# Skewness of 1024 rows: the last block's cubes written over their squares in PSUM, and the closing arithmetic moved from VectorE to ScalarE

## The chip, the cores and the metric

One NeuronCore of a Trainium2 chip. The metric is the device time of one execution in microseconds (us). A profiled execution gives a span, which is some 1.8 us shorter than the time, and a trace. Short names: PE is TensorE, DVE is VectorE, ACT is ScalarE, POOL is GpSimd. SBUF and PSUM are the core's two on-chip memories. A semaphore is a counter on which an instruction waits until another is done; a self-wait is such a wait of an engine for its own earlier instruction. An instruction that also gives a sum (accum_out) has a second record behind it in the trace, its accumulator read; the sum is ready when that ends. A pointer operand is a number per row, read from a 128x1 tile.

Ratios below are the mean time of one kernel's fast runs over the mean time of the kernel before in the same rounds on the same chip, with a 95% interval. They are not quite the ratio of the medians that stand beside them.

## The reference

```python
x = randn(1024, 8192)            # float32
mean = x.mean(-1, keepdims=True)
std  = x.std(-1, keepdims=True)
z = (x - mean) / (std + 1e-8)
out = (z ** 3).mean(-1)          # 1024 numbers
```

With the raw moments m1, m2, m3 (means of x, x^2, x^3) this is (m3 - 3 m1 m2 + 2 m1^3) / var^1.5, with var = m2 - m1^2. The kernel reads the 33.55 MB of x once.

## The kernel before

The rows lie in eight blocks of 128 partitions. Each block comes in several column units, each unit in one or more slices. For every slice ACT squares x and accumulates the sum of squares, and DVE multiplies the square by x and accumulates the sum of cubes. PE transposes x and adds it up, for the mean. From the last unit of block 6 on, the squares lie in PSUM in two buffers in turn (psq). The cube itself is wanted by nobody, only its sum, so it is written to a scratch tile called cube; in earlier blocks it goes over its square (sq).

```python
cube = small("cube", PS_MAX)                # one tile in SBUF
...
act(out=sq, in_=xt[:, s:e], func=AF.Square, scale=s_scale,
    accum_out=s2u[:, j : j + 1])
nc.vector.scalar_tensor_tensor(
    out=cube[:, 0 : e - s] if (b, k) >= PSUM_FROM else sq,
    in0=sq, scalar=1.0, in1=xt[:, s:e],
    op0=ALU.mult, op1=ALU.mult, accum_out=s3u[:, j : j + 1])
...
# the end, for block 7; p1 = m1 in PSUM
g.tensor_tensor(out=m2, in0=m2p, in1=s2u[:, j - 1 : j], op=ALU.add)
act(out=m1sq, in_=p1, func=AF.Square)
g.tensor_tensor(out=var, in0=m2, in1=m1sq, op=ALU.subtract)
g.tensor_tensor(out=rr, in0=var, in1=expo[:, 0:1], op=ALU.pow)
act(out=nm1, in_=p1, func=AF.Copy, scale=-3.0)
act(out=v3, in_=m1sq, func=AF.Identity, scale=1.0 / 3.0, bias=var)
nc.vector.tensor_reduce(out=num, in_=s3u[...block 7...], axis=X_AXIS, op=ALU.add)
nc.vector.scalar_tensor_tensor(out=num, in0=v3, scalar=nm1, in1=num,
                               op0=ALU.mult, op1=ALU.add)
nc.vector.tensor_tensor(out=skew[:, L:NB], in0=num, in1=rr, op=ALU.mult)
nc.sync.dma_start(out=ov, in_=skew)
```

The names in the trace drop digits: v3 is v_l, m2 is m_l, nm1 is nm_l, n3 is n_l there, num is num_l, and so on.

Of the kernel before, what the change touches and what calls it, by code (L numbers as in the profile page):

```python
# [9 lines left out]
AF = mybir.ActivationFunctionType  # L10
ALU = mybir.AluOpType
X_AXIS = mybir.AxisListType.X
# [12 lines left out]
PSUM_FROM = (6, 5)  # L25
SUB_MAX = 2304
PS_MAX, PS_BUFS = 1536, 2
# [12 lines left out]
def _plan(b, k):  # L40
    return _slices(UNITS[b][k], PS_MAX if (b, k) >= PSUM_FROM else SUB_MAX)


@with_exitstack
def kernel(
    ctx: ExitStack,
    tc: tile.TileContext,
    x: bass.AP,
    out: bass.AP,
):  # L50
    nc = tc.nc
    eng = mybir.EngineType
    ctx.enter_context(tc.manual_schedule(
        engines={eng.PE, eng.Activation, eng.DVE, eng.Pool, eng.SP}))
    P = nc.NUM_PARTITIONS
    R, C = x.shape
    NB = R // P
    L = NB - 1
    F = EARLY
    inv_n = 1.0 / float(C)  # L60
    s_scale = float(C) ** -0.5
    third = (1.0 / 3.0) ** 0.5
    assert len(UNITS) == NB and all(sum(u) == C for u in UNITS) and F == L


    xv = x.rearrange("(p b) c -> b p c", b=NB)
    ov = out.rearrange("(p b) -> p b", b=NB)


    n_sl = [sum(len(_plan(b, k)) for k in range(len(u))) for b, u in enumerate(UNITS)]  # L70
    K = max(n_sl)

    xpool = ctx.enter_context(tc.tile_pool(name="xp", bufs=X_BUFS))
    sqpool = ctx.enter_context(tc.tile_pool(name="sqp", bufs=SQ_BUFS))
    onep = ctx.enter_context(tc.tile_pool(name="onep", bufs=1))
    psq = ctx.enter_context(tc.tile_pool(name="psq", bufs=PS_BUFS, space=bass.MemoryType.PSUM))
    psum1 = ctx.enter_context(tc.tile_pool(name="ps1", bufs=1, space=bass.MemoryType.PSUM))

    def small(name, n):
        return onep.tile([P, n], FP, tag=name, name=name)  # L80

    onesn = small("onesn", 1)
    nc.vector.memset(onesn, inv_n)  # L83
    tiny = small("tiny", 1)
    nc.scalar.activation(out=tiny, in_=onesn, func=AF.Square)  # L85
    ident = small("ident", P)
    make_identity(nc, ident)
    s2u = small("s2u", NB * K)
    s3u = small("s3u", NB * K)
    nc.vector.memset(s2u, 0.0)  # L90
    nc.vector.memset(s3u, 0.0)
    cube = small("cube", PS_MAX)
    junk = small("junk", K)
    expo = small("expo", F)
    nc.gpsimd.memset(expo, -1.5)
    skew = small("skew", NB)
    m1a = small("m1a", F)
    tsb = small("tsb", P)

    tp = psum1.tile([P, P], FP, tag="tp", name="tp")  # L100
    s1ps = psum1.tile([P, NB], FP, tag="s1ps", name="s1ps")
    act, g = nc.scalar.activation, nc.gpsimd

    def close_first_blocks():

        m2, m3 = small("m2a", F), small("m3a", F)
        for dst, src in ((m2, s2u), (m3, s3u)):
            nc.vector.tensor_reduce(  # L108
                out=dst, in_=src[:, 0 : F * K].rearrange("p (b c) -> p b c", c=K),
                axis=X_AXIS, op=ALU.add,  # L110
            )
        m1sq, m1sq3, nm1 = small("m1sqa", F), small("m1sq3a", F), small("nm1a", F)
        act(out=m1sq, in_=m1a, func=AF.Square)
        act(out=m1sq3, in_=m1a, func=AF.Square, scale=third)
        act(out=nm1, in_=m1a, func=AF.Copy, scale=-3.0)
        var, rr = small("vara", F), small("rra", F)
        g.tensor_tensor(out=var, in0=m2, in1=m1sq, op=ALU.subtract)  # L117
        g.tensor_tensor(out=m1sq3, in0=m1sq3, in1=var, op=ALU.add)
        g.tensor_tensor(out=m1sq3, in0=m1sq3, in1=nm1, op=ALU.mult)
        g.tensor_tensor(out=m3, in0=m3, in1=m1sq3, op=ALU.add)  # L120
        g.tensor_tensor(out=rr, in0=var, in1=expo, op=ALU.pow)  # L121
        g.tensor_tensor(out=skew[:, 0:F], in0=m3, in1=rr, op=ALU.mult)

    for b, widths in enumerate(UNITS):
        c0 = 0
        j = b * K
        for k, w in enumerate(widths):
            last_unit = b == L and k == len(widths) - 1
            xt = xpool.tile([P, w], FP, tag="x", name=f"x_{b}_{k}")
            nc.sync.dma_start(out=xt, in_=xv[b, :, c0 : c0 + w])  # L130
            c0 += w
            n = w // P
            for c in range(n):
                nc.tensor.matmul(  # L134
                    out=tp, lhsT=xt[:, c * P : (c + 1) * P], rhs=ident,
                    start=(k == 0 and c == 0), stop=(c0 == C and c == n - 1),
                    is_transpose=True,
                )
            if last_unit:
                nc.scalar.copy(out=tsb, in_=tp)  # L140
            for s, e in _plan(b, k):
                if (b, k) >= PSUM_FROM:
                    sq = psq.tile([P, PS_MAX], FP, tag="psq", name=f"psq_{b}_{k}_{s}")[:, 0 : e - s]
                else:
                    sq = sqpool.tile([P, e - s], FP, tag="sq", name=f"sq_{b}_{k}_{s}")
                act(  # L146
                    out=sq, in_=xt[:, s:e], func=AF.Square, scale=s_scale,
                    accum_out=s2u[:, j : j + 1],
                )
                nc.vector.scalar_tensor_tensor(  # L150
                    out=cube[:, 0 : e - s] if (b, k) >= PSUM_FROM else sq,
                    in0=sq, scalar=1.0, in1=xt[:, s:e],
                    op0=ALU.mult, op1=ALU.mult, accum_out=s3u[:, j : j + 1],
                )
                j += 1
            if (b, k) == EARLY_AT:
                nc.scalar.copy(out=m1a, in_=s1ps[:, 0:F])
                close_first_blocks()
            if b == L and k == len(widths) - 2:
                m2p = small("m2p", 1)  # L160
                act(out=junk[:, 0 : n_sl[L] - 1], in_=s2u[:, L * K : j], func=AF.Copy,
                    accum_out=m2p)
        if b < L:
            nc.scalar.copy(out=tsb, in_=tp)  # L164
        nc.tensor.matmul(out=s1ps[:, b : b + 1], lhsT=tsb, rhs=onesn, start=True, stop=True)  # L165


    p1 = s1ps[:, L : L + 1]
    m1sq, nm1, v3, m2, var, rr, num = (
        small(f"{t}_l", 1) for t in ("m1sq", "nm1", "v3", "m2", "var", "rr", "num")  # L170
    )
    g.tensor_tensor(out=m2, in0=m2p, in1=s2u[:, j - 1 : j], op=ALU.add)
    act(out=m1sq, in_=p1, func=AF.Square)
    g.tensor_tensor(out=var, in0=m2, in1=m1sq, op=ALU.subtract)  # L174
    g.tensor_tensor(out=rr, in0=var, in1=expo[:, 0:1], op=ALU.pow)  # L175
    act(out=nm1, in_=p1, func=AF.Copy, scale=-3.0)
    act(out=v3, in_=m1sq, func=AF.Identity, scale=1.0 / 3.0, bias=var)  # L177
    nc.vector.tensor_reduce(out=num, in_=s3u[:, L * K : L * K + n_sl[L]], axis=X_AXIS, op=ALU.add)  # L178
    nc.vector.scalar_tensor_tensor(  # L179
        out=num, in0=v3, scalar=nm1, in1=num, op0=ALU.mult, op1=ALU.add  # L180
    )
    nc.vector.tensor_tensor(out=skew[:, L:NB], in0=num, in1=rr, op=ALU.mult)  # L182
    nc.sync.dma_start(out=ov, in_=skew)


# [28 lines left out]
```

## Time and profile before

| | before |
|---|---|
| time, median of 3 | 92.33 us (92.21 to 92.37) |
| span of the profiled run | 90.6 us |
| x has landed by | about 83.4 us |
| last cube's sum ready | 87.51 us |
| last DVE step ends | 88.30 us |

The prediction shows the lines. ACT waits for x for the last time at 78.76 us, PE at 83.41. From the fourth cube of block 7 (82.04 us) to the end DVE works without waiting for data, so that stretch is what a change of the tail can shorten.

### The profile page before, as it was taken

The page shows a single profiled execution, that of the slowest core. Times are in us where ns is not written, and L with a number is a line of the kernel's source. Part 1 is how long each engine was busy: PE and PEld are TensorE (multiplying, and loading weights), DVE is VectorE, ACT ScalarE, POOL GpSimd, SP SyncE. Part 2 cuts the span into 40 slices and gives each one's busy share as a digit, 9 for nine tenths or more (in the row PEclk, how much of TensorE's full clock was granted, in tenths as well). Part 3 has the DMA queues.
Part 4 walks back from the last instruction along what each step waited for, and adds up shares of the span by engine and source line. Part 5 has one row for each costly group of instructions (what it writes and reads, how often), then busy time and mean ns, then how long its engine had stood idle before and what let it go on. Part 6 is the DMA issues. An engine that isn't in the chain of part 4 may idle for free. (4 is left out here: it accounts for less than half of the span.)

```text
span 90.6 us, 1442 instructions
## 1 busy us (share of the span) xinstructions
PE 66.5 (73%) x528; PEld 60.2 (66%) x528; DVE 74.1 (82%) x92; ACT 69.1 (76%) x103; POOL 4.2 (5%) x16
## 2 busy tenths in 40 slices
PE   0003999988986959897589778989898798897700
PEld 0003999887975949686569667978687586776600
DVE  0000498969999799999988999999999989989980
ACT  6003969497885979897589889989888798898910
POOL 3000000000000000000000000000000000006440
PEclk9999999999999999999999999999999999999996
DMA  3999999999999999999999999999999999992000
GB/s 101 347 412 427 441 427 420 434 449 430 397 407 442 419 432 426 420 428 418 422 421 433 411 426 411 409 410 420 411 416 420 409 411 421 412 397 115 0 0 2
DMA packets 4614, 33.64 MB, mean 371 GB/s; under 512 B 640, under 2 KB 640, under 8 KB 3072
## 3 DMA queue, kind: packets, MB, share of 16 engines
q1 hardware_dynamic: 4608, 33.56, 89.4%
q8 instruction: 4, 0.07, 0.3%
q14 instruction: 2, 0.02, 0.0%
HBM read 33.55 MB, written 0.00 MB: 370 GB/s over the span
## 5 line engine op out<-in xcount | busy, mean ns | idle before, releaser
L134 PE MATMUL tp<-ident,x 128*128 128x128 f32 x512 | 64.0, 282 | 16.0 <-DMA x<-in_x_dram 15.8
L150 DVE SCALAR_TENSOR_TENSOR sq<-sq,x 128x2048 f32<-128x2048 f32 (+9 forms) x34 | 62.0, 1872 | 12.4 <-ACT sq L146 12.3
L134 PEld LDWEIGHTS tp<-ident,x 128*128 128x128 f32 x512 | 58.3, 146 | 20.3 <-DMA x<-in_x_dram 11.9
L146 ACT ACTIVATE sq<-x 128x2048 f32<-128x2048 f32 (+9 forms) x34 | 53.5, 1575 | 14.4 <-DMA x<-in_x_dram 12.6
L150 DVE SCALAR_TENSOR_TENSOR cube<-psq,x 128x1280 f32<-128x1280 f32 (+3 forms) x8 | 11.1, 1390 | 0.7 <-ACT psq L146 0.2
L146 ACT ACTIVATE psq<-x 128x1280 f32<-128x1280 f32 (+3 forms) x8 | 9.3, 1161 | 0.9 <-DVE cube L150 0.5
L146 ACT ACTIVATION_READ_ACCUMULATOR sq<-x 128x1 f32 x34 | 6.3, 186 | 0.0
L165 PEld LDWEIGHTS s1ps<-onesn,tsb 128*128 128x128 f32 x16 | 2.4, 188 | 5.2 <-ACT tsb L164 4.7
L165 PE MATMUL s1ps<-onesn,tsb 128*128 128x1 f32 x16 | 3.1, 260 | 3.4 <-ACT tsb L164 3.0
L117 POOL TENSOR_TENSOR vara<-m2a,m1sqa 128x7 f32<-128x7 f32 x1 | 0.2, 206 | 80.8 <-DVE m3a L108 80.8
L150 DVE DVE_READ_ACCUMULATOR sq<-sq,x 128x1 f32 x34 | 2.8, 82 | 0.0
L164 ACT COPY tsb<-tp 128x128 f32<-128x128 f32 x7 | 1.7, 250 | 1.3 <-PE tp L134 1.2
L85 ACT ACT_TABLE_LOAD x1 | 1.3, 1283 | 0.7 <-PEq L198 0.7
L121 POOL TENSOR_TENSOR rra<-vara,expo 128x7 f32<-128x7 f32 x1 | 1.5, 1507 | 0.0
L146 ACT ACTIVATION_READ_ACCUMULATOR psq<-x 128x1 f32 x8 | 1.5, 188 | 0.0
L83 DVE MEMSET onesn<- 128x1 f32 x1 | 0.1, 59 | 0.8 <-PEq L198 0.8
L150 DVE DVE_READ_ACCUMULATOR cube<-psq,x 128x1 f32 x8 | 0.7, 84 | 0.0
L177 ACT ACTIVATE v_l<-m1sq_l,var_l 128x1 f32<-128x1 f32 x1 | 0.3, 294 | 0.4 <-POOL var_l L174 0.4
L175 POOL TENSOR_TENSOR rr_l<-var_l,expo 128x1 f32<-128x1 f32 x1 | 0.6, 563 | 0.1
L179 DVE SCALAR_TENSOR_TENSOR num_l<-v_l,nm_l,num_l 128x1 f32<-128x1 f32 x1 | 0.2, 220 | 0.1
masks.py:199 POOL TENSOR_SCALAR_AFFINE_SELECT ident<-ident 128x128 f32<-128x128 f32 x1 | 0.3, 294 | 0.1
L140 ACT COPY tsb<-tp 128x128 f32<-128x128 f32 x1 | 0.3, 266 | 0.0
(27 smaller groups left out, 4.5 us busy)
## 6 DMA issues: line engine op xcount, KB each, us to landing
x<-in_x_dram SPq DMA_DIRECT2D x4, 2048.0 KB, 14.1
x<-in_x_dram SPq DMA_DIRECT2D x4, 1472.0 KB, 27.2
x<-in_x_dram SPq DMA_DIRECT2D x5, 640.0 KB, 9.3
x<-in_x_dram SPq DMA_DIRECT2D x4, 704.0 KB, 10.1
x<-in_x_dram SPq DMA_DIRECT2D x2, 960.0 KB, 19.8
x<-in_x_dram SPq DMA_DIRECT2D x2, 896.0 KB, 22.6
x<-in_x_dram SPq DMA_DIRECT2D x1, 1728.0 KB, 25.4
x<-in_x_dram SPq DMA_DIRECT2D x2, 768.0 KB, 15.2
```

Of the source, the lines that this page charges most:

```text
L85: nc.scalar.activation(out=tiny, in_=onesn, func=AF.Square)
L117: g.tensor_tensor(out=var, in0=m2, in1=m1sq, op=ALU.subtract)
L121: g.tensor_tensor(out=rr, in0=var, in1=expo, op=ALU.pow)
L134: nc.tensor.matmul(out=tp, lhsT=xt[:, c * P : (c + 1) * P], rhs=ident, start=(k == 0 and c == 0), stop=(c0 == C and c == n - 1), is_transp ...
L140: nc.scalar.copy(out=tsb, in_=tp)
L146: act(out=sq, in_=xt[:, s:e], func=AF.Square, scale=s_scale, accum_out=s2u[:, j : j + 1],)
L150: nc.vector.scalar_tensor_tensor(out=cube[:, 0 : e - s] if (b, k) >= PSUM_FROM else sq, in0=sq, scalar=1.0, in1=xt[:, s:e], op0=ALU.mult, ...
L164: nc.scalar.copy(out=tsb, in_=tp)
L165: nc.tensor.matmul(out=s1ps[:, b : b + 1], lhsT=tsb, rhs=onesn, start=True, stop=True)
L175: g.tensor_tensor(out=rr, in0=var, in1=expo[:, 0:1], op=ALU.pow)
L177: act(out=v3, in_=m1sq, func=AF.Identity, scale=1.0 / 3.0, bias=var)
L179: nc.vector.scalar_tensor_tensor(out=num, in0=v3, scalar=nm1, in1=num, op0=ALU.mult, op1=ALU.add)
```

## The change

It means to shorten the tail at both ends. Cubes of block 7 (and the last of block 6) go over their squares, so the scratch tile and the waits of DVE for itself disappear. And DVE keeps one step behind the last cube instead of three: ACT adds up the earlier cube sums (n3) and forms num = -3 m1 v3 + n3, and DVE finishes with (last sum + num) * rr. To make room on ACT the partial sum of squares moves one unit earlier, at the price of one more addition on POOL.

```diff
-    cube = small("cube", PS_MAX)
...
-                    out=cube[:, 0 : e - s] if (b, k) >= PSUM_FROM else sq,
+                    out=sq,
...
-            if b == L and k == len(widths) - 2:
+            if b == L and k == len(widths) - 3:
                 m2p = small("m2p", 1)
-                act(out=junk[:, 0 : n_sl[L] - 1], in_=s2u[:, L * K : j], func=AF.Copy,
+                act(out=junk[:, 0 : n_sl[L] - 2], in_=s2u[:, L * K : j], func=AF.Copy,
                     accum_out=m2p)
...
+    g.tensor_tensor(out=m2p, in0=m2p, in1=s2u[:, j - 2 : j - 1], op=ALU.add)
     g.tensor_tensor(out=m2, in0=m2p, in1=s2u[:, j - 1 : j], op=ALU.add)
...
-    nc.vector.tensor_reduce(out=num, in_=s3u[:, L * K : L * K + n_sl[L]], axis=X_AXIS, op=ALU.add)
-    nc.vector.scalar_tensor_tensor(
-        out=num, in0=v3, scalar=nm1, in1=num, op0=ALU.mult, op1=ALU.add
+    n3 = small("n3_l", 1)
+    act(out=junk[:, 0 : n_sl[L] - 1], in_=s3u[:, L * K : j - 1], func=AF.Copy, accum_out=n3)
+    act(out=num, in_=v3, func=AF.Identity, scale=nm1, bias=n3)
+    nc.vector.tensor_scalar(
+        out=skew[:, L:NB], in0=s3u[:, j - 1 : j], scalar1=num, scalar2=rr,
+        op0=ALU.add, op1=ALU.mult,
     )
-    nc.vector.tensor_tensor(out=skew[:, L:NB], in0=num, in1=rr, op=ALU.mult)
```

## The prediction

> **What bounds the kernel now.** I read the page first, for where the engines stand.
>
> ```profile
> span 90.6 us, 1442 instructions
> PE 66.5 (73%) x528; PEld 60.2 (66%) x528; DVE 74.1 (82%) x92; ACT 69.1 (76%) x103; POOL 4.2 (5%) x16
> DMA  3999999999999999999999999999999999992000
> GB/s 101 347 412 427 441 427 420 434 449 430 397 407 442 419 432 426 420 428 418 422 421 433 411 426 411 409 410 420 411 416 420 409 411 421 412 397 115 0 0 2
> ```
>
> The DMA row is the one to see: 35 slices of 2.27 us full, at about 420 GB/s, and then nothing. No engine reaches that. So until about 83.5 us the arrival of x sets the pace, and work saved on DVE before then is lost in a wait for data. What a tail change can move is the stretch after the last landing, roughly 83.4 to 90.6 us. Second, the timeline of that stretch (columns: start, duration, engine, line, operation, tiles, then idle before it and who ended it).
>
> ```profile
> 82.04 1.48 DVE L150 SCALAR_TENSOR_TENSOR cube<-psq,x 128x1280 f32<-128x1280 f32 x1
> 83.62 1.49 DVE L150 SCALAR_TENSOR_TENSOR cube<-psq,x 128x1280 f32<-128x1280 f32 x1
> 84.74 0.19 ACT L146 ACTIVATION_READ_ACCUMULATOR psq<-x 128x1 f32 x1
> 85.19 0.27 ACT L140 COPY tsb<-tp 128x128 f32<-128x128 f32 x1
> 85.21 1.49 DVE L150 SCALAR_TENSOR_TENSOR cube<-psq,x 128x1280 f32<-128x1280 f32 x1
> 85.36 0.61 ACT L146 ACTIVATE psq<-x 128x512 f32<-128x512 f32 x1
> 85.89 0.19 ACT L146 ACTIVATION_READ_ACCUMULATOR psq<-x 128x1 f32 x1
> 86.65 0.29 ACT L177 ACTIVATE v_l<-m1sq_l,var_l 128x1 f32<-128x1 f32 x1 [0.45 <-POOL var_l L174]
> 86.70 0.56 POOL L175 TENSOR_TENSOR rr_l<-var_l,expo 128x1 f32<-128x1 f32 x1
> 86.80 0.69 DVE L150 SCALAR_TENSOR_TENSOR cube<-psq,x 128x512 f32<-128x512 f32 x1
> 87.42 0.08 DVE L150 DVE_READ_ACCUMULATOR cube<-psq,x 128x1 f32 x1
> 87.54 0.16 DVE L178 TENSOR_REDUCE num_l<-s3u 128x1 f32<-128x7 f32 x1
> 87.82 0.22 DVE L179 SCALAR_TENSOR_TENSOR num_l<-v_l,nm_l,num_l 128x1 f32<-128x1 f32 x1
> 88.14 0.16 DVE L182 TENSOR_TENSOR skew<-num_l,rr_l 128x1 f32<-128x1 f32 x1
> 88.33 0.35 SPq L183 DMA_DIRECT2D out_dram<-skew  x1
> ```
>
> DVE sets the end. The last four cubes start at 82.04, 83.62, 85.21 and 86.80, with no stall but a small gap before each. Then three tiny steps run from 87.54 to 88.30, the output is issued at 88.33, and 2.3 us later the span ends. The square of the last unit is there at 86.08 (85.89 + 0.19), 0.72 us before its cube begins, so ACT has slack. The chain of waits agrees: nothing but DVE.
>
> To price the gap I looked at cubes of the same width in an earlier block, where the cube already overwrites its square.
>
> ```profile
> 54.02 1.48 DVE L150 SCALAR_TENSOR_TENSOR sq<-sq,x 128x1280 f32<-128x1280 f32 x1
> 55.43 1.48 DVE L150 SCALAR_TENSOR_TENSOR sq<-sq,x 128x1280 f32<-128x1280 f32 x1
> 56.85 0.08 DVE L150 DVE_READ_ACCUMULATOR sq<-sq,x 128x1 f32 x1
> ```
>
> Start to start is 1.41 us there, against 1.58 to 1.59 in block 7, though the instruction lasts the same 1.48 to 1.49. The instruction streams say why. All cubes of block 7 write one tile, cube, so each carries a wait on DVE's own semaphore for the one before it. Cubes that write sq carry none, and begin under the end of their predecessor. So the self-wait costs 1.59 - 1.41 = 0.18 us.
>
> **What the Trainium skill says.** "VectorE: DVE Perf Modes", section "The DRAIN you can't avoid", reports that eight copies take the same 13.88 us with a semaphore after each as with one after the last. By that the self-wait would be free. This trace differs (1.59 against 1.41 us), and I follow the trace. "Perfetto Trace Analysis", section "Optimizing Scalar/DVE Operations", gives a DVE access overhead of about 60 ns on SBUF and 125 ns on PSUM. For a PSUM read the trace hardly shows it (1489 ns mean from psq, 1484 ns from sq, both 1280 wide); no cube writes PSUM yet, so up to 65 ns more each is an open estimate. "PSUM — Partial Sum Buffer", section "PSUM bank collisions raise a hardware error", forbids two engines in one bank at a time. A psq buffer is 1536 x 4 bytes, three of that page's 2 KiB banks, so ACT's buffer and DVE's share none; on one engine reading and writing the same bank the section is silent, and so is this trace. "ScalarE: Activation LUTs", section "What ACT_TABLE_LOAD costs", adds about 93 ns for each per-partition scale or bias operand, and lets neighbours overlap by about 93 ns. The trace: v3 with one such operand took 294 ns, its neighbours without one 163 and 173; and the three small squares and copies from 80.31 on start 0.12, 0.10 and 0.09 us apart at 190 to 208 ns each. It agrees within some 30 ns.
>
> **The change, part by part.**
>
> Part one, cubes over squares. Seven self-waits vanish, those of block 7 (0.18 x 7 = 1.26 us of DVE time at most). I walk it. The first cube of block 7 can begin at 75.49 + 1.41 = 76.90 instead of 77.08. The second is held by its square, ready at 78.40, so 78.42 instead of 78.53. The third waits for its square, which waited for the DMA (78.76 to 80.24), so 80.26 as before: what was gained is lost here. The two reductions of the closing of blocks 0 to 6 follow at 81.81 and 81.93, without waits, and the fourth cube stays at 82.04. From here DVE is behind its squares. Fifth: 82.04 + 1.41 = 83.45 (before 83.62). Sixth: 83.45 + 1.41 = 84.86, but its square ends its accumulator read at 84.93, so 84.95 (before 85.21). Seventh: 84.95 + 1.41 = 86.36 (before 86.80), its square being there at 86.08. Its sum is ready at 86.36 + 0.71 = 87.07 instead of 87.51. So three waits count, and of 0.53 us the square of the sixth unit takes 0.09: 0.44 us.
>
> Part two, the second moment. The partial sum of squares moves one unit earlier on ACT, to about 83.33, in front of the sixth square. ACT idled 0.27 us there for a buffer, until 83.56. At its old place the sum delayed its successor by 0.23 us (84.96 to 85.19), so 83.33 + 0.23 = 83.56 and the square is not moved. Nothing is won at its old place: the copy of tp at 85.19 waits for the last transpose too. That began at 84.88; in block 0, where the copy visibly waited for PE, it followed its last transpose's start by 0.31 us (17.82 to 18.13), and 84.88 + 0.31 = 85.19. So the last square stays at 85.36 to 86.08. The extra POOL addition (0.19 us, spaced 0.27) has its input by 84.93 and POOL is free from 84.96 to 86.16, so it is hidden, and var, v3 and rr stay at 86.62, 86.65 to 86.94 and 87.26.
>
> Part three, the end. DVE's three steps go, 88.30 - 87.51 = 0.79 us. In their place one step of DVE, and two of ACT behind v3. The sum n3 needs the sixth cube's sum (84.95 + 1.49 = 86.44, there in time) and starts at 86.65 + 0.29 - 0.09 = 86.85; its accumulator read starts 0.11 later as at 84.96 and ends at 86.96 + 0.19 = 87.15. num waits for it (0.03, as at 84.93 to 84.96), starts at 87.18, and with two pointer operands lasts 0.29 + 0.10 = 0.39, to 87.57. The DVE step can then start. It has two pointer operands; the step with pointers before it in the old tail began 0.12 us after its predecessor's end (87.70 to 87.82) and took 0.22. Taking 0.05 to 0.12 for the start and 0.16 to 0.22 for the step, it ends at 87.78 to 87.91, say 87.85.
>
> Sum: 88.30 - 87.85 = 0.45 us earlier, the issue and the 2.3 us behind it unchanged. 92.33 - 0.45 = 91.88 us, 0.5%. The gain is not 0.44 + 0.57, because ACT is the later of the two inputs, by 0.5 us (87.57 against DVE's 87.07): DVE's tail is halved only to wait for ACT.
>
> **The rivals.** First, DVE stays the bound: a cube into PSUM starts no earlier than today, because the write costs as much as the wait did. Then its sum is at 87.51, the last step starts at about 87.6, just where ACT's chain lets it, and the time is the same 91.9. If only up to 65 ns a cube is lost, ACT hides it wholly. So the result hardly depends on part one. Second, reading and writing one PSUM bank from one engine runs at half rate. Nothing speaks for it but that no cube does it yet; the eight cubes take 11.1 us, and the last four, which count, 5.15; doubled, they would give about 97 us. Third, ACT's chain is longer than I add up, say each link by 0.05 to 0.1, with five links: the gain falls to 0.1 or 0.2, 92.15. Fourth, the sums pile up as the author may hope, ACT's two steps fitting beside DVE's last cube, with the end at 87.07 + 0.3: 91.4. Against it speaks that v3 cannot begin before var at 86.62, whatever DVE does.
>
> **Range and chances.** Link errors of ACT's chain give about +-0.2 us, and the three runs of before spread over 0.16. So 91.6 to 92.2 for 8 in 10. Faster by over 2% would need 1.85 us, more than the whole tail of small steps plus every self-wait on the path (0.79 + 0.53): 1%. Slower by over 2% is the half-rate rival: 2%. Within 2%: 97%.
>
> **What would show it.** Right if: cubes of 1280 in block 7 stay near 1.49 us and start 1.41 apart from the fourth on; the third and fourth still start near 80.26 and 82.04; the last cube's sum is ready near 87.1; the last DVE step waits for ACT, not for DVE, and ends near 87.85; the chain of waits now passes through ACT's num and n3 and POOL's var. Wrong if the cubes last over 1.6 us, if the sixth square or the copy of tp move by more than 0.1 us, or if the last step waits for the last cube.

## More of the kernel before

One line is POOL's addition for m2 in the timeline of the kernel before (start, duration, engine, line, operation, tiles, then the idle time before it and who ended it).

```profile
86.16 0.19 POOL L172 TENSOR_TENSOR m_l<-m2p,s2u 128x1 f32<-128x1 f32 x1 [1.20 <-ACT m1sq_l L173]
```

## The result, and the profile after

The changed kernel took 91.95 us (91.92 to 92.01, 4 runs) against 92.35 us (92.21 to 92.44) of the kernel before in the same rounds: ratio 0.9959, interval 0.9942 to 0.9976. That is 0.4 us, clear of noise and far within 2%.

First the chain of waits of the changed kernel: its summary by engine, and pieces from its end (start, length, what).

```profile
DMA 77%; ACT 8%; SPq 4%; PE 3%; issue 2%; DVE 2%; POOL 0%; DVEq 0%; POOLq 0%; ACTq 0%
...
83.38 1.76 PE tp L133 x14
...
85.32 0.72 ACT psq L145 x2
...
86.45 0.20 POOL var_l L174
...
86.68 0.29 ACT v_l L177
86.97 0.20 ACT junk L180 x2
...
87.19 0.40 ACT num_l L181
...
87.68 0.27 DVE skew L182
```

Before, this chain held DVE alone, but it could be followed back only to 86.71 us. Now it leads from the last step back through num and n3 to v3, all on ACT, and through POOL (var, m2), ACT (the last square) and PE (the last transposes of x) to the DMA. Second, the timeline of the tail:

```profile
83.43 1.53 DVE L149 SCALAR_TENSOR_TENSOR psq<-psq,x 128x1280 f32<-128x1280 f32 x1
85.00 1.50 DVE L149 SCALAR_TENSOR_TENSOR psq<-psq,x 128x1280 f32<-128x1280 f32 x1
85.85 0.19 ACT L145 ACTIVATION_READ_ACCUMULATOR psq<-x 128x1 f32 x1
86.19 0.19 POOL L172 TENSOR_TENSOR m_l<-m2p,s2u 128x1 f32<-128x1 f32 x1 [0.95 <-ACT nm_l L176]
86.42 0.73 DVE L149 SCALAR_TENSOR_TENSOR psq<-psq,x 128x512 f32<-128x512 f32 x1
87.06 0.14 DVE L149 DVE_READ_ACCUMULATOR psq<-psq,x 128x1 f32 x1
87.68 0.27 DVE L182 TENSOR_SCALAR skew<-s3u,num_l,rr_l 128x1 f32<-128x1 f32 x1 [0.48 <-ACT num_l L181]
```

The fifth, sixth and seventh cube start at 83.43, 85.00 and 86.42 instead of 83.62, 85.21 and 86.80. The last sum is ready at 87.20 (87.06 + 0.14) instead of 87.51. DVE then idles 0.48 us and waits for num, which ends at 87.58. The last step ends at 87.95 instead of 88.30.

As a yardstick that depends little on when x happened to land in the profiled run, take the **stretch** from the start of the fourth cube of block 7 to the end of the last DVE step: 88.30 - 82.04 = 6.26 us before, 87.95 - 82.02 = 5.93 us after.

### The profile page after: what moved, and what is told of

The parts are those of the page before. It is cut to its first block, busy times and chain, and to the rows that moved or that the text cites. A ratio compares the mean times of both kernels' runs of the same rounds, so it can differ in the third digit from the quotient of the medians.

```text
span 90.2 us, 1444 instructions
## 1 busy us (share of the span) xinstructions
PE 66.6 (74%) x528; PEld 60.3 (67%) x528; DVE 73.9 (82%) x90; ACT 69.7 (77%) x106; POOL 4.4 (5%) x17
## 4 chain that ended last, share of the span: by engine, by line
DMA 77%; ACT 8%; SPq 4%; PE 3%; issue 2%; DVE 2%; POOL 0%; DVEq 0%; POOLq 0%; ACTq 0%
DMA x<-in_x_dram 77%; ACT sq L145 6%; SPq L129 4%; PE tp L133 3%; DVE sq L149 2%; ACT psq L145 1%; ACT num_l L181 0%; ACT v_l L177 0%; DVE skew L182 0%; ACT junk L180 0%; POOL var_l L174 0%; POOL m_l L172 0%; ACT nm_l L176 0%; ACT m1sq_l L173 0%; DVEq L182 0%
## 5 line engine op out<-in xcount | busy, mean ns | idle before, releaser
L149 DVE SCALAR_TENSOR_TENSOR psq<-psq,x 128x1280 f32<-128x1280 f32 (+3 forms) x8 | 11.0, 1409 | 0.4 <-ACT psq L145 0.2
L149 DVE DVE_READ_ACCUMULATOR psq<-psq,x 128x1 f32 x8 | 1.1, 140 | 0.0
```

The source lines that it names most:

```text
L149: nc.vector.scalar_tensor_tensor(out=sq, in0=sq, scalar=1.0, in1=xt[:, s:e], op0=ALU.mult, op1=ALU.mult, accum_out=s3u[:, j : j + 1],)
```

## The experiments

My theory (A): before, DVE set the end, and a wait for itself cost it 0.18 us per cube; before about 82 us that is swallowed by the arrival of x. Now ACT's chain behind the last square sets the end, so DVE's gain is partly idle. Its rivals in the expectations: B, only the new end gives the gain; B', the gains of the two parts add up; C, every self-wait that is removed gives its share. D is no rival of A: it says that the moved partial sum costs a little instead of paying.

| run | median us | ratio to before (95%) | stretch us |
|---|---|---|---|
| changed kernel | 91.95 | 0.9959 (0.9942 to 0.9976) | 5.93 |
| cubes_in_place | 91.97 | 0.9973 (0.9961 to 0.9986) | 5.98 |
| tail_alone | 91.86 | 0.9960 (0.9948 to 0.9973) | 5.95 |
| cubes_two_tiles | 91.76 | 0.9947 (0.9935 to 0.9958) | 5.83 |
| v3_from_m2 | 91.67 | 0.9937 (0.9925 to 0.9948) | 5.68 |
| in_place_late | 91.98 | 0.9965 (0.9952 to 0.9977) | 5.99 |
| in_place_early | 92.20 | 0.9996 (0.9984 to 1.0009) | 6.26 |
| m2_old_place | 91.84 | 0.9955 (0.9942 to 0.9969) | 5.89 |
| all_together | 91.49 | 0.9916 (0.9903 to 0.9930) | 5.58 |
| changed_again | 92.02 | 0.9968 (0.9955 to 0.9980) | 5.96 |
| m2_old_again | 91.97 | 0.9957 (0.9944 to 0.9969) | 5.88 |
| last_step_one_pointer | 91.94 | 0.9963 (0.9949 to 0.9976) | 5.88 |

The medians of before were 92.25, 92.30 and 92.34 us in the three calls (rows 2 to 5, 6 to 9, 10 to 12).

For the kernels with the new end there is a sharper measure: from the start of the last transpose of x on PE, on which ACT's chain hangs, to the end of the last DVE step. It is 3.10 us in the changed kernel (84.85 to 87.95), 3.11 in changed_again, 3.10 in tail_alone, 2.83 in v3_from_m2, 3.05 and 3.04 in m2_old_place and m2_old_again, 3.06 in last_step_one_pointer and 2.73 in all_together.

**cubes_in_place** is the first part alone.

```diff
 kernel before
-    out=cube[:, 0 : e - s] if (b, k) >= PSUM_FROM else sq,
+    out=sq,
```

> Only the cubes of block 7 over their squares in PSUM; the old end with three DVE steps and the old place of the partial second moment. Theory A (self-waits were on the path while DVE set the end; with the new end ACT sets it): the last cube's sum is ready near 87.2 us as in the changed kernel, the three DVE steps follow it in 0.79 us, gain 0.30 us, about 92.05. Theory B (the gain of the change is the new end alone, the self-waits were hidden): no gain, 92.35.

It took 0.9973 of before, 0.28 us off the stretch. Theory B falls: the self-waits were on the path. With three DVE steps behind it, the earlier last sum counts in full.

**tail_alone** is the rest of the change alone.

```diff
 changed kernel
-    out=sq,
+    out=cube[:, 0 : e - s] if (b, k) >= PSUM_FROM else sq,
```

> Only the new end: cubes of block 7 go into one SBUF tile again, with their waits on DVE itself. Theory A: the last cube's sum comes at 87.5, still before ACT's num at 87.58, so the whole gain stays: 91.95 to 92.0, same as the changed kernel. Theory B' (the parts add: 0.3 from the self-waits and 0.1 from the end): 92.25.

It gave 0.9960, the whole gain of the change without its first part. From the timeline of this run:

```profile
87.03 0.39 ACT L182 ACTIVATE num_l<-v_l,n_l,nm_l 128x1 f32<-128x1 f32 x1
87.22 0.08 DVE L150 DVE_READ_ACCUMULATOR cube<-psq,x 128x1 f32 x1
87.52 0.27 DVE L183 TENSOR_SCALAR skew<-s3u,num_l,rr_l 128x1 f32<-128x1 f32 x1 [0.22 <-ACT num_l L182]
```

DVE's sum is late again (87.30), but num ends at 87.42 and still comes last. Only DVE's idle time shrinks, from 0.48 to 0.22 us. So the two parts do not add: each alone takes 0.28 and 0.31 us off the stretch, both together 0.33. B' falls.

**cubes_two_tiles** takes the self-wait away without touching PSUM.

```diff
 kernel before
-    cube = small("cube", PS_MAX)
+    cubes = [small(f"cube{i}", PS_MAX) for i in range(2)]
-    out=cube[:, 0 : e - s] if (b, k) >= PSUM_FROM else sq,
+    out=cubes[(j + b) % 2][:, 0 : e - s] if (b, k) >= PSUM_FROM else sq,
```

> The kernel before with two cube tiles in SBUF in turn instead of one: same destination memory, no wait of DVE on itself. If the wait is what costs (theory A): cubes of 1280 start 1.41 us apart, accumulator reads stay 0.08 us (PSUM cubes had 0.14), the last sum is ready at 87.07 to 87.1, gain 0.40 us, 91.93. If the destination was what mattered: spacing stays 1.59, no gain, 92.35.

The instruction stream now has no wait of these cubes on DVE's own semaphore. It shows in the semaphore instructions that DVE's sequencer handles for the cubes from 81 to 87 us (count; shortest, median and longest ns; first and last start), first in the kernel before, then here:

```profile
L150 DVEq EVENT_SEMAPHORE  x4: 1473/1495/1646, 80.3 to 85.3; - x4
L150 DVEq EVENT_SEMAPHORE  x3: 21/21/21, 81.8 to 84.8; - x3
```

Before, each lasts about as long as the cube that it waits for; here all are over at once. And the timeline shows cubes of 1280 columns 1.41 us apart where ACT does not hold them (81.81 to 83.22):

```profile
81.81 1.48 DVE L150 SCALAR_TENSOR_TENSOR cube<-psq,x 128x1280 f32<-128x1280 f32 x1
83.22 1.49 DVE L150 SCALAR_TENSOR_TENSOR cube<-psq,x 128x1280 f32<-128x1280 f32 x1
```

So the wait was what cost, not the memory the cube went to. This version even beats the first part of the change (0.9947 against 0.9973, the intervals do not overlap), by 0.15 us of stretch. The groups of the changed kernel by shape (count, busy us, mean ns) say where that goes:

```profile
L149 DVE DVE_READ_ACCUMULATOR psq<-psq,x 128x1 f32 x8 | 1.1, 140 | 0.0
L149 DVE SCALAR_TENSOR_TENSOR psq<-psq,x 128x512 f32<-128x512 f32 x1 | 0.7, 731 | 0.0
```

With cubes into SBUF tiles these groups take 83 and 685 ns in cubes_two_tiles. With the cube in PSUM the accumulator read behind it is 57 ns longer. That accounts for 0.10 us at the last cube and its read. The other 0.06 us comes through ACT: its sixth square needs the buffer of the fourth cube and starts 0.03 us behind that cube's accumulator read in both runs, so the sixth cube is later too (2.98 us behind the fourth in cubes_in_place, 2.92 here).

**in_place_late** and **in_place_early** split the first part at the fourth cube of block 7, with the old end.

```diff
 kernel before, late
-    out=cube[...] if (b, k) >= PSUM_FROM else sq,
+    out=cube[...] if PSUM_FROM <= (b, k) < (L, 3) else sq,
 kernel before, early
+    out=cube[...] if (b, k) >= (L, 3) else sq,
```

> The old end; only the last four cubes over their squares, so only the self-waits behind the fourth cube of block 7 go. Theory A (before about 82 us the arrival of x swallows what DVE saves): the whole gain of all cubes in place with the old end, 0.25 to 0.3 us, about 0.997 of before. Theory C (each removed self-wait of 0.18 us gives its share): three of seven, about 0.12 us, 0.9987.

> The old end; the first four cubes of block 7 and the one before them over their squares, the last four into one SBUF tile with their waits on DVE itself. Theory A: the third cube still starts with its late square, the fourth behind the two reductions, and the end does not move: 1.000 of before. Theory C: four of seven shares, about 0.16 us, 0.998.

Late gave 0.9965, all of it; early 0.9996, nothing. Theory C falls. The timeline of the early run shows why: though the first cubes run without self-waits, the square of the third unit waits for x, DVE stands 0.23 us idle before the third cube, and the stretch from the fourth on is as long as before (6.26 us).

```profile
78.58 1.35 ACT L146 ACTIVATE psq<-x 128x1408 f32<-128x1408 f32 x1 [0.32 <-DMA x<-in_x_dram]
80.08 1.63 DVE L150 SCALAR_TENSOR_TENSOR psq<-psq,x 128x1408 f32<-128x1408 f32 x1 [0.23 <-ACT psq L146]
81.85 1.48 DVE L150 SCALAR_TENSOR_TENSOR cube<-psq,x 128x1280 f32<-128x1280 f32 x1
```

**v3_from_m2** shortens ACT's chain and leaves DVE as it is. As var = m2 - m1^2, v3 = var + m1^2/3 = m2 - 2/3 m1^2, which needs one POOL step less.

```diff
 changed kernel
-    act(out=v3, in_=m1sq, func=AF.Identity, scale=1.0 / 3.0, bias=var)
+    act(out=v3, in_=m1sq, func=AF.Identity, scale=-2.0 / 3.0, bias=m2)
```

> The changed kernel with v3 taken as m2 - 2/3 m1^2 instead of var + 1/3 m1^2, the same value one POOL step earlier. Theory A (ACT's chain behind var sets the end): v3 starts at 86.41 instead of 86.68, num ends near 87.3, the end moves 0.27 us forward, 91.68. If DVE's last cube or POOL's rr set the end: no change, 91.95.

It took 91.67 us, ratio 0.9937; the stretch fell by 0.25 us. Its timeline:

```profile
86.25 0.29 ACT L177 ACTIVATE v_l<-m1sq_l,m_l 128x1 f32<-128x1 f32 x1 [0.24 <-POOL m_l L172]
87.24 0.27 DVE L182 TENSOR_SCALAR skew<-s3u,num_l,rr_l 128x1 f32<-128x1 f32 x1 [0.23 <-ACT num_l L181]
```

One POOL step (0.27 us from m2's start to var's) taken out of ACT's chain moved the end by as much: 0.27 us, counted from the last transpose (3.10 to 2.83). So the chain over POOL and ACT, and not DVE, sets the end of the changed kernel. In this run rr, POOL's other result, is ready 0.03 us before num.

**m2_old_place**, **changed_again** and **m2_old_again** ask what the moved partial sum is worth. The edit puts it back behind the sixth square and drops the extra POOL addition.

```diff
 changed kernel
-    if b == L and k == len(widths) - 3:
+    if b == L and k == len(widths) - 2:
-    act(out=junk[:, 0 : n_sl[L] - 2], ...)
+    act(out=junk[:, 0 : n_sl[L] - 1], ...)
-    g.tensor_tensor(out=m2p, in0=m2p, in1=s2u[:, j - 2 : j - 1], op=ALU.add)
```

> The changed kernel with the partial second moment back at its old place and without the second POOL addition. In the changed kernel the POOL step for m2 waits for two semaphores and starts 0.15 us behind the last square's accumulator read, before it was 0.08 with one. Theory D (this second wait costs on ACT's path, the moved sum gives nothing as the copy of tp waits for PE anyway): 0.04 to 0.07 us faster than the changed kernel, about 0.995 of before. If moving the sum paid: 0.1 us slower than the changed kernel, 0.997.

> The changed kernel itself, so that the next two can be compared with it on one chip in the same rounds: 0.996 of before, in the trace 5.93 us from the start of the fourth cube of block 7 to the end of the last DVE step.

> The same edit as in m2_old_place. Theory D: 0.04 us less than the changed kernel in the trace measured from the fourth cube (5.89 against 5.93 us), 0.03 to 0.07 us in time, about 0.9955 of before. If the place of the sum is of no account: equal to the changed kernel within 0.02 us in the trace.

In the traces theory D holds. POOL's addition for m2 starts 0.15 us behind the last square's accumulator read in the changed kernel (86.04 to 86.19); with the old place it is 0.08 again (85.88 to 85.96), as in the kernel before (86.08 to 86.16):

```profile
85.96 0.19 POOL L171 TENSOR_TENSOR m_l<-m2p,s2u 128x1 f32<-128x1 f32 x1 [1.21 <-ACT m1sq_l L172]
```

In the changed kernel m2 waits for ACT and for POOL's own addition, and the trace has a semaphore instruction of POOL's sequencer (17 ns) of that line, which the old place does not have. "Perfetto Trace Analysis", section "Identifying Dependency Chains", in the Trainium skill says that such instructions may be put ahead of one that waits on several engines; here that goes with some 0.06 us. The gap is the same 0.14 to 0.15 us in all five kernels with the second POOL addition, and 0.08 in all eight without it. In time the difference is at the edge: 0.9957 against 0.9968 in the same rounds, overlapping intervals. The stretch says 0.04 to 0.08 us in favour of the old place; counted from the last transpose it is 0.06 us in both pairs (3.10 and 3.11 against 3.05 and 3.04). The device time agrees but is too coarse to prove it.

**last_step_one_pointer** looks at the one term of my sum that came out too small.

```diff
 changed kernel
-    nc.vector.tensor_scalar(out=skew[:, L:NB], in0=s3u[:, j - 1 : j],
-        scalar1=num, scalar2=rr, op0=ALU.add, op1=ALU.mult)
+    nc.vector.scalar_tensor_tensor(out=skew[:, L:NB], in0=s3u[:, j - 1 : j],
+        scalar=num, in1=rr, op0=ALU.add, op1=ALU.mult)
```

> The changed kernel, its last DVE step with num as a pointer operand and rr as a tensor operand instead of two pointers. If the second pointer is what made the step longer than predicted: 0.22 us instead of 0.27, the start behind num unchanged at 0.09 to 0.10, the end 0.05 us earlier, about 0.9955 of before. If the step's length has another cause: 0.27 us, no change.

```profile
87.62 0.22 DVE L182 SCALAR_TENSOR_TENSOR skew<-s3u,num_l,rr_l 128x1 f32<-128x1 f32 x1 [0.47 <-ACT num_l L181]
```

The step fell from 0.27 to 0.22 us, with the same start 0.10 us behind num. The time (0.9963 against 0.9968) is too coarse to show 0.05 us. The edit changes the instruction along with the pointer, so "one pointer less" is the likely cause and not an isolated one. The last small steps on DVE with none, one and two pointer operands took 0.16, 0.22 and 0.27 us in these runs, but they are three different instructions.

**all_together** is the version to keep: two SBUF tiles for the cubes, the new end, v3 from m2, the sum at its old place, one pointer in the last step. All five edits stand above.

> Cubes of block 7 into two SBUF tiles in turn, the new end, v3 from m2, the old place of the partial second moment, and the last DVE step with one pointer operand and one tensor operand instead of two pointers. If A and D hold and the last step falls from 0.27 to 0.22 us: v3_from_m2's 0.9937 less 0.06 and 0.05 us, about 0.9925 of before. If DVE's sum or rr takes over as the bound: 0.9935 or more.

It took 91.49 us (91.43 to 91.58), ratio 0.9916 (0.9903 to 0.9930): twice the gain of the change, and better than both kernels. Its timeline:

```profile
86.43 0.56 POOL L175 TENSOR_TENSOR rr_l<-var_l,expo 128x1 f32<-128x1 f32 x1
86.64 0.39 ACT L181 ACTIVATE num_l<-v_l,n_l,nm_l 128x1 f32<-128x1 f32 x1
86.72 0.08 DVE L150 DVE_READ_ACCUMULATOR cube<-psq,x 128x1 f32 x1
87.13 0.22 DVE L182 SCALAR_TENSOR_TENSOR skew<-s3u,num_l,rr_l 128x1 f32<-128x1 f32 x1 [0.32 <-ACT num_l L181]
```

The three inputs of the last step now come within a quarter of a microsecond: DVE's sum at 86.80, rr at 86.99, num at 87.03. There is little left to move between the engines. Counted from the last transpose the end came 0.37 us earlier than in the changed kernel (3.10 to 2.73), about the sum of the three cuts in ACT's chain and behind it: 0.27 for v3, 0.06 for the sum's place, 0.05 for the last step.

## Why the prediction was right

The forecast was 91.88 us with 91.6 to 92.2; measured were 91.95 in the first rounds and 92.02 in the last. By its steps:

- **What swallows the gain of the first cubes.** Right in the step by step account: the third cube started at 80.25 and the fourth at 82.02 (forecast 80.26 and 82.04), and the early split gained nothing. The reading at its head was wrong: the DMA row is full to 81.5 us and not to 83.5, and savings on DVE count from the fourth cube at 82.04 on, not from the last landing.
- **The self-wait of 0.18 us, three of which count.** Right in mechanism: two SBUF tiles remove it and bring spacing down to 1.41 us. The fifth to seventh cube came at 83.43, 85.00 and 86.42 (forecast 83.45, 84.95, 86.36). The forecast of 87.07 for the last sum was 0.13 us early: the last cube began 0.06 late (the sixth square started at 83.60, not 83.56, behind the longer accumulator read of the fourth cube), it lasted 0.73 instead of 0.69 us and its accumulator read 0.14 instead of 0.08, both with PSUM as destination. That is what became of the open estimate of up to 65 ns for each cube written to PSUM: the spacing stayed 1.41 us, the reads took 57 ns more. It did not matter, as ACT came later.
- **The moved partial sum, worth nothing.** Nearly right. The copy of tp followed the start of its last transpose by 0.31 us with the moved sum and by 0.31 to 0.34 us with the old place, so at most 0.03 us was won. What I missed is that m2, with a second semaphore to wait for, starts 0.15 instead of 0.08 us behind the square; I had called the extra addition hidden. That is 0.03 us on my absolute time of m2 (86.19 against 86.16).
- **ACT's chain.** Right to 0.03 us: v3 at 86.68 (86.65), n3 summed by 87.16 (87.15), num from 87.19 to 87.58 (87.18 to 87.57). The estimate of one more pointer operand, about 0.1 us, measured 387 - 294 = 93 ns, which is what "ScalarE: Activation LUTs", section "What ACT_TABLE_LOAD costs", in the Trainium skill gives.
- **The last DVE step.** The mis-sized term: 0.27 us against 0.16 to 0.22 that I allowed from the old steps, with a start 0.10 us behind num, within the allowed 0.05 to 0.12. It makes up most of the 0.10 us by which the end came late (87.95 against 87.85). So the gain of 0.45 us came out as 0.33 us of stretch, and as 0.30 to 0.38 us by the ratios of the two measurements.
- **The rivals.** That the result hardly depends on the first part is shown by tail_alone. Half rate in PSUM is out: cubes of 1280 last 1502 ns instead of 1489. The author's hope, both tails overlapping, fails at var as argued: taking var out of v3 moved the end by 0.27 us.

## What to carry to other kernels

When the end of a kernel is fed by several engines, write down when each input of the last instruction is ready: shortening the latest pays until the next one is reached, and here two parts worth 0.28 and 0.31 us alone gave 0.33 together. A scratch output that nobody reads should not be one single tile: each writer then waits for the one before it, 0.18 us a time here, and a second tile is cheaper than another memory. Before moving work to another engine, look whether the algebra lets that engine start one step earlier; that gave 0.25 us for one changed line.

## What the Trainium skill lacked or had wrong

- "VectorE: DVE Perf Modes", section "The DRAIN you can't avoid", has a semaphore after each op cost nothing; it measured eight tensor copies. Here a cube (a scalar_tensor_tensor with an accumulator output) that waits for its predecessor's semaphore starts 1.59 us behind it instead of 1.41 (1280 columns), and taking away the waits alone gained 0.5% of the time.
- "PSUM — Partial Sum Buffer", section "PSUM bank collisions raise a hardware error", does not say what one engine reading and writing the same bank costs. Here DVE does it at nearly the same rate: 1502 ns against 1487 with an SBUF destination at 1280 columns; the accumulator read behind it takes 140 instead of 83 ns.
- "Perfetto Trace Analysis", section "Identifying Dependency Chains", names the semaphore instruction ahead of an instruction with several waits but gives no cost. Here a POOL step with it started 0.15 us behind its last input instead of 0.08.
